# Pair 2's gather moved ahead of the overflow check, mean squares taken in column groups, and one more pair of experts stored and gathered, in a one-core hybrid decoder block

## The chip, the cores and the metric

The kernel runs on one core of a Trainium2 chip. The metric is the device time of one execution in microseconds (us). The kernel before took 687.26 us, the median of three runs (685.65 to 687.46). The profile is of one execution, in which every instruction of the five engines has a record: PE (TensorE, the matmuls; PEld is its weight load), DVE (VectorE), ACT (ScalarE), POOL (GpSimd) and SP (SyncE, which here issues DMAs and computes nothing).

## The reference, cut to what matters

One decoder layer works on 512 tokens of width 1024, in float32:

```
h = rms_norm(x);  z = h @ w_in                      # 1024 x 4864
y_r = retention(...) @ w_ret_o;  q, k = rms_norm per head of 64;  y_s = swa(q, k, v) @ w_swa_o
x = x + (sigmoid(gate_r) * y_r + sigmoid(gate_s) * y_s) @ w_out
x = x + sum over the token's 2 experts of w * (silu(n @ Wg) * (n @ Wu)) @ Wd   # n = rms_norm(x)
x = x + sigmoid(rms_norm(x) @ w_ple_gate) * rms_norm(p @ w_ple)
```

There are 32 experts of width 256. Each token goes to two of them, so there are 1024 pairs of a token and an expert, 64 on average for two experts. The per-head norms of q (8 heads) and k (2 heads) need the mean square over 64 columns of each of 10 heads.

## The kernel before, in words

**First part (0 to about 310 us).** The projections run as "units" of 128 columns with three matmuls for each block of 128 inputs (a rounded high part and a low remainder of both operands, `mm_T`, L441). A planner orders the instructions of this part by its own costs. Attention (`swa`, L534) and retention are generators whose steps are laid between the units. The first step of `swa` sums the squares of q and k over each head: five matmuls (L540) with the squares of two heads each write into the same 10 partitions of a PSUM bank, DVE copies the 10 rows out (L544), PE transposes them (L546, four blocks), DVE adds epsilon (L550), and POOL raises the 2 k columns and the 8 q columns to the power -0.5 (L554, L555). Two matmul rows later (L562) PE spreads the k factors.

**From L1104 on** the order of the instructions on every engine is the written order of the program; nothing is reordered, and an engine that waits holds everything behind it.

**Router and expert pairs.** Experts are handled in 16 pairs (p and p + 16). Each of the two has 64 slots, so a pair has 128 rows. For a pair, in this order: `gu` (L1187) multiplies the pair's rows by gate and up weights, with the two experts in the two halves of PE's columns (L1195); `hidden` (L1204) makes silu times up; `ht` (L1212) transposes it (L1216); `turn` (L1080) transposes the rows of the next pair (L1087), which an indirect DMA on POOL has gathered from X1 in DRAM (`fetch`, L1071, DMA on L1076), and then issues the gather of two pairs ahead; `turned` puts the norm's gain on them (DVE, L976); `down` (L1224) multiplies by the down weights (L1239). The weights, 6 MB for a pair, come by DMAs that SP issues in one fixed order as slabs of SBUF come free (`pump`, L310; the DMAs are L336 and L338). They go around eight semaphores in turn.

**Overflow check.** In pair 0, between `gu(0)` and `hidden(0)`, `overflow` (L1325) reads the largest number of tokens of an expert into a register (L1333, L1337) and branches: where an expert has over 64 tokens, the rest is worked off in a loop; here the branch isn't taken. The block inside uses some slabs as scratch: unit 8 for its weights (`wb`), and units 0 and 4, which hold the weights `gu(1, 1)` and `gu(17, 1)`, and so are loaded again at the block's end. When the branch isn't taken, SP waits in turn for each of the eight semaphores and raises it by what the block would have added (nine event instructions on L1337). `fetch(1)` stands ahead of the check. `fetch(2)` writes unit 8 and stands behind the check (L1565).

**Bringing results back to the tokens.** Pairs 0 to 11 (`SC = 12`) are stored: the 128 rows of `down` go to DRAM by an indirect DMA (L1259). At pair 12, `collect` (L1512) clears eight buffers on POOL (L1517) and gathers each token's stored rows (L1522, eight indirect DMAs); rows of pairs not stored are skipped. POOL adds the two rows of a token (`presum`, L1529), for blocks 0 and 1 at the end of pair 13, for blocks 2 and 3 at the end of pair 14; DVE adds them to the residual (`total`, L1534), for blocks 0 and 1 at the end of pair 14, and for 2 and 3 in the tail. Pairs 12 to 15 are "combined" instead: `down` rounds its rows into a high and a low part (L1249, L1250), DVE builds a one-hot matrix (L1232), and in the next pair PE multiplies both parts by it for each of four token blocks (`combine`, L1269: 4 matmuls a block, 16 a pair), and DVE adds the bank to the residual (`added`, L1282). Block 3 of pair 14 is combined in the tail with block 3 of pair 15.

**Tail.** For each token block: `combine([15], t)` and, for blocks 2 and 3, `total`; `tail_a` transposes the residual on PE (L1449) and splits it (L1451, L1453, L1455); `tail_b` multiplies by the gate weights (L1475); `tail_c` ends the block and stores it. The gate weights are split ahead of that (`wpsplit`, L1419) in four pieces: ACT makes the high part (L1427) and POOL, for the first three pieces, the low part (L1429), two POOL instructions a piece. Pieces 0 and 1 come in pair 15, piece 2 behind `tail_a(0)`. The written order at the seam is:

```
down(15); total / presum of that pair, if any
combine([15], 0); tail_a(0); wpsplit(2); combine([15], 1); tail_b(0, 0); wpsplit(3)
```

Of the kernel before, what the change touches and what calls it, by code (L numbers as in the profile page):

```python
# [13 lines left out]
OP = mybir.AluOpType  # L14
AX = mybir.AxisListType

P = 128
# [10 lines left out]
def constants():  # L28

    p = np.arange(P, dtype=np.float64)  # L30
    lg = np.log1p(-np.exp2(-5.0 - np.arange(4)))
    parts = []

    def add(name, a):
        a = np.broadcast_to(np.asarray(a, dtype=np.float64), (P,) + np.shape(a)[1:])
        parts.append((name, a.reshape(P, -1)))

    add("id", np.eye(P))
    add("mh", np.full((P, 40), -0.5))
    add("blk", np.stack([np.stack([((p // 64) == m - 2 * i) / 64.0 for m in range(10)], 1) for i in range(5)], 1))  # L40
    add("ones", np.ones((P, P)))
    add("up", (p[:, None] < p[None, :]) * 1.0)
    ij = p[None, :] >= p[:, None]
    dk = 128.0 ** -0.5
    rm = (np.stack([np.where(ij, np.exp(-(p[:, None] + 1) * lg[h]), 0.0) * dk for h in range(4)], 1))
    xi = np.tile(np.stack([np.exp((p + 1) * lg[h]) for h in range(4)])[None], (P, 1, 1))
    add("zeta", np.stack([np.exp((127.0 - p) * lg[h]) * dk for h in range(4)], 1))
    add("io64", (np.arange(SLOTS) + 1.0)[None])
    add("io32", np.arange(NE)[None] * 1.0)
    add("dst", np.stack([k * S + t * P + p - BIG for k in range(2) for t in range(4)], 1))  # L50
    off, o = {}, 0
    for n, a in parts:
        off[n] = (o, o + a.shape[1])
        o += a.shape[1]
    tab = np.concatenate([a for _, a in parts], 1).astype(np.float32)
    q = np.arange(P)
    s = np.arange(2 * P)
    rel = q[:, None] + P - s[None, :]
    ok = (rel >= 0) & (rel < P)
    sl = np.exp2(-np.arange(1, 9, dtype=np.float64))  # L60
    bias = np.stack([np.where(ok, -sl[h] * rel, -1e30) for h in range(8)], 1).astype(np.float32)
    return tab, off, bias, rm.reshape(P, 512).astype(np.float32), xi.reshape(P, 512).astype(np.float32)
# [136 lines left out]
def program(tc, I, out):  # L199
    nc = tc.nc  # L200
    V, A, T, G, Q = nc.vector, nc.scalar, nc.tensor, nc.gpsimd, nc.sync
# [18 lines left out]
    def C(name, a=0, b=None):  # L220
        lo, hi = CO[name]
        return ct[:, lo + a: hi if b is None else lo + b]
# [27 lines left out]
    LN = 256  # L250
    FW = ((0, 1), ), ((1, 2), (2, 4))
    TB0 = 0
    SC = 12
    KEEP = {7: (42, 50), 9: (42, 74)}
    AT = {("gu", 1, 0): 14, ("gu", 17, 0): 18, ("gu", 1, 1): 0, ("gu", 17, 1): 4}
    LATE = (("gu", 17, 1),)
# [277 lines left out]
    def swa():  # L534
# [1 line left out]
        qH, qL, kraw, vS = z["qH"], z["qL"], z["kraw"], z["vS"]  # L536
        aH, aL = ar.get(8, r=True), ar.get(8, r=True)
        pm, p2 = bgb(), bgb()
        for i in range(5):
            T.matmul(pm[0:10, :], C("blk", 10 * i, 10 * i + 10), sq2[i].f(512), start=(i == 0), stop=(i == 4))  # L540
        for s_ in sq2:
            s_.free()
        mr = ar.get(2, "t")
        V.tensor_copy(mr.f(512)[0:10, :], pm[0:10, :])  # L544
        for t in range(4):
            T.transpose(p2[:, t * 10:t * 10 + 10], mr.f(4, P)[0:10, t, :], ident[0:10, 0:10])  # L546
        mr.free()
        r = small(40)
        rk_ = small(8)
        V.tensor_tensor(r.rearrange("p (t c) -> p t c", t=4), p2[:, 0:40].rearrange("p (t c) -> p t c", t=4),  # L550
                        em[:, :, None].to_broadcast([P, 4, 10]), op=OP.add)
        rv4, rk4 = r.rearrange("p (t c) -> p t c", t=4), rk_.rearrange("p (t c) -> p t c", t=4)
        mh = C("mh", 0, 40).rearrange("p (t c) -> p t c", t=4)
        G.tensor_tensor(rk4, rv4[:, :, 8:10], mh[:, :, 8:10], op=OP.pow)  # L554
# [724 lines left out]
    def added(t):  # L1279
        for nh in range(2):  # L1280
            xs = x2[t].f(1024)[:, nh * 512:(nh + 1) * 512]
            V.tensor_tensor(xs, xs, CB[t][nh], op=OP.add)  # L1282
# [41 lines left out]

    def overflow():  # L1325

        spill = [(key, loaded.pop(key)) for key in (("gu", 1, 1), ("gu", 17, 1))]
        for _, a in spill:
            a.free()
        gm, tb_, xg, h, xr, wb = (ar.get(kb, r=r, at=at) for kb, r, at in (  # L1330
            (2, True, 0), (4, False, 1), (4, False, 4), (2, False, 3), (4, False, 6), (4, False, 8)))
        o = xr
        count = lambda ap: nc.values_load(ap, min_val=0, max_val=S, skip_runtime_bounds_check_because=(  # L1333
            "a token counts once for an expert, so 512 is the most"))
# [203 lines left out]
    for p_ in range(16):  # L1538
# [6 lines left out]
        if p_ == 0:  # L1545
            gu(0, range(2))
            post_e(2), post_e(3)
            for t in range(4):
                G0[t].free()
            tables()  # L1550
            fetch(1)
            counts()
            gu(0, range(2, 4))
        else:
            gu(p_, range(4))
# [6 lines left out]
            overflow()  # L1562
        hidden(p_)
        if p_ == 0:
            fetch(2)  # L1565
            ht(0)
            down(0)
            pump(0)
            turned(1, turn(1))
            continue  # L1570
# [4 lines left out]
        ht(p_)  # L1575
        if p_ > SC:
            added(2)
        turned(p_ + 1, turn(p_ + 1))
        for t in range(4):
            if PU[t] == p_:  # L1580
# [28 lines left out]
    tail_c(0, 1)  # L1609
    for t in range(1, 4):  # L1610
        if t < 3:
            combine([15] if t == 1 else [14, 15], t + 1)
            total(t + 1)
        tail_b(t, 0)
        tail_c(t, 0)
        if t < 3:
            tail_a(t + 1)
            tail_r(t + 1)
        for lo in range(0, 512, 512 if t < 3 else LN):
            tail_b(t, 1, lo, 512 if t < 3 else LN)  # L1620
            tail_c(t, 1, lo, 512 if t < 3 else LN)
# [59 lines left out]
```

## Time and profile before

| | |
|---|---|
| median of the runs shown | 687.26 us |
| the profiled execution's own time | 686.33 us |
| its span, first to last instruction | 684.6 us |
| PE busy | 649.4 us (95%) |
| PEld, DVE, ACT, POOL busy | 440.2, 317.0, 201.4, 99.1 us |
| DMA | 162.98 MB, mean 238 GB/s |
| granted PE clock, mean over the span | 0.995 of full speed |

A span is the time from the first to the last instruction. Times in the rows below are us from the span's start, unless a mean of one instruction is given in ns. A row of a timeline has the start, the time, the engine, the line, the operation, the tiles written and read, the shape and the count of merged instructions; in brackets stands the idle time before it and what ended that. Line numbers are those of the kernel before.

### The profile page before, as it was taken

To read this page: it belongs to the slowest core of one execution; us is meant where nothing else is said; L and a number is where in the kernel's file an instruction comes from. 1 tells how busy PE (TensorE), PEld (TensorE's weight loads), DVE (VectorE), ACT (ScalarE), POOL (GpSimd) and SP (SyncE) were. 2 spreads that over 40 slices of the span, in tenths; PEclk is the share of its full clock that TensorE was granted. 3 is DMA by queue.
4 is the path that set the end of the run, shared out by engine and by line. 5 is a ranking of instruction groups with operands and counts; after the bars stand their busy time and mean duration, and the time that the engine had idled before them with its cause. 6 is when DMAs were issued, how large, how long until landed. Compare 5 with 4: busy or idle time off the path is not lost. (4 is left out here: it accounts for less than half of the span.)

```text
span 684.6 us, 8420 instructions
## 1 busy us (share of the span) xinstructions
PE 649.4 (95%) x3210; PEld 440.2 (64%) x3210; DVE 317.0 (46%) x689; ACT 201.4 (29%) x393; POOL 99.1 (14%) x83
## 2 busy tenths in 40 slices
PE   8999999999999999999998879899999999898997
PEld 6868888778888888888888323333333443344886
DVE  5595545662456425634157312222122236565863
ACT  6764253462143334440142000000211110005431
POOL 2014000000001000000000021111421118226300
PEclk9999999999999999999999989999999999999999
DMA  8727310531304731045899759999999999994011
GB/s 279 302 78 277 108 62 2 183 124 63 117 20 170 309 123 62 0 185 202 354 402 371 287 185 371 418 419 419 421 421 419 376 423 417 417 416 197 32 47 46
DMA packets 32476, 162.98 MB, mean 238 GB/s; under 512 B 5577, under 2 KB 8265, under 8 KB 16304
## 3 DMA queue, kind: packets, MB, share of 16 engines
q1 hardware_dynamic: 26672, 149.90, 55.5%
q0 software_dynamic: 5040, 10.39, 4.0%
q10 hardware_dynamic: 720, 2.11, 0.8%
q8 instruction: 26, 0.43, 0.2%
q14 instruction: 18, 0.15, 0.1%
HBM read 155.67 MB, written 14.68 MB: 249 GB/s over the span
## 5 line engine op out<-in xcount | busy, mean ns | idle before, releaser
L445 PE MATMUL bank<-slab,slab 128*128 128x512 f32 x320 | 126.3, 395 | 0.0
L446 PE MATMUL bank<-slab,slab 128*128 128x512 f32 x320 | 125.0, 391 | 0.0
L447 PE MATMUL bank<-slab,slab 128*128 128x512 f32 x320 | 124.9, 391 | 0.0
L1195 PE MATMUL bank<-slab,slab 128*64 128x512 f32 x512 | 121.4, 595 | 2.2 <-issue 1.0
L1195 PEld LDWEIGHTS bank<-slab,slab 128*64 128x64 f32 x512 | 37.9, 137 | 78.9 <-issue 70.0
L362 DVE TENSOR_TENSOR slab<-slab,slab 128x1024 fp32r<-128x1024 f32 (+2 forms) x50 | 54.0, 1093 | 57.2 <-ACT slab L361 42.4
L445 PEld LDWEIGHTS bank<-slab,slab 128*128 128x128 f32 x320 | 60.1, 188 | 13.9 <-issue 1.8
L447 PEld LDWEIGHTS bank<-slab,slab 128*128 128x128 f32 x320 | 60.1, 188 | 12.8 <-DVE slab L362 0.3
L446 PEld LDWEIGHTS bank<-slab,slab 128*128 128x128 f32 x320 | 60.2, 188 | 11.7
L1239 PE MATMUL bank<-slab,slab 128*64 128x512 f32 x256 | 61.3, 612 | 2.3 <-DMA slab<-wd 1.7
L361 ACT ACTIVATE slab<-slab 128x1024 fp32r<-128x1024 f32 (+2 forms) x50 | 46.4, 952 | 56.7 <-PE bank L446 25.4
L1209 DVE SCALAR_TENSOR_TENSOR slab<-slab,st,bank 128x256 f32<-128x256 f32 x16 | 7.7, 480 | 99.9 <-ACT slab L1208 99.9
L1208 ACT ACTIVATE slab<-bank,st 128x256 f32<-128x256 f32 x16 | 7.6, 474 | 138.1 <-PE bank L1195 130.4
L1475 PE MATMUL bank<-slab,slab 128*128 128x512 f32 (+1 forms) x216 | 45.3, 368 | 0.0
L1475 PEld LDWEIGHTS bank<-slab,slab 128*128 128x128 f32 x216 | 37.1, 189 | 6.8 <-ACT slab L1453 0.3
L1239 PEld LDWEIGHTS bank<-slab,slab 128*64 128x64 f32 x256 | 18.6, 140 | 34.5 <-issue 32.2
L1076 POOL DMA_INDIRECT slab<-X,st x15 | 15.5, 1034 | 83.0 <-PE bank L1195 49.7
L369 POOL TENSOR_TENSOR st<-st,ct 128x4 f32<-128x4 f32 x4 | 4.4, 1102 | 159.3 <-DVE st L368 159.3
L894 PE MATMUL bank<-slab,slab 128*128 128x512 f32 x64 | 26.1, 408 | 0.0
L896 PE MATMUL bank<-slab,slab 128*128 128x512 f32 x64 | 25.0, 391 | 0.0
L895 PE MATMUL bank<-slab,slab 128*128 128x512 f32 x64 | 24.9, 390 | 0.0
L1252 DVE COPY slab<-bank 128x512 f32<-128x512 f32 x12 | 8.3, 692 | 32.0 <-PE bank L1239 32.0
(248 smaller groups left out, 926.4 us busy)
## 6 DMA issues: line engine op xcount, KB each, us to landing
slab<-wgu SPq DMA_DIRECT2D x64, 1024.0 KB, 14.8
slab<-wd SPq DMA_DIRECT2D x31, 1024.0 KB, 16.5
slab<-win SPq DMA_DIRECT2D x17, 1024.0 KB, 4.9
slab<-x SPq DMA_DIRECT2D x8, 512.0 KB, 6.2
Y<-slab SPq DMA_DIRECT2D x8, 512.0 KB, 5.4
slab<-wout SPq DMA_DIRECT2D x4, 1024.0 KB
slab<-wpg SPq DMA_DIRECT2D x4, 1024.0 KB, 22.4
slab<-wso SPq DMA_DIRECT2D x2, 1024.0 KB, 6.6
```

The lines of the kernel that those rows point to most:

```text
L361: A.activation(H.r(*shape), rawap, AF.Copy)
L362: (eng or V).tensor_tensor(L.r(*shape), rawap, H.f(*shape), op=OP.subtract)
L445: T.matmul(ps, wh[:, k, :], hh[k], start=(k == 0), stop=False)
L446: T.matmul(ps, wh[:, k, :], hl[k], start=False, stop=False)
L447: T.matmul(ps, wl[:, k, :], hh[k], start=False, stop=(k == nk - 1))
L894: T.matmul(ps, a, wh[:, kk, :], start=(k == 0), stop=False)
L895: T.matmul(ps, a, wl[:, kk, :], start=False, stop=False)
L896: T.matmul(ps, b, wh[:, kk, :], start=False, stop=(k == 7))
L1076: G.indirect_dma_start(out=XR[p_].f(1024), out_offset=None, in_=X1, in_offset=bass.IndirectOffsetOnAxis(ap=toki[:, p_:p_ + 1], axis=0), bo ...
L1195: T.matmul(b[j * 64:(j + 1) * 64, :], xg[:, k, j * 64:(j + 1) * 64], load(("gu", p_ + 16 * j, k // 4)).f(4, 512)[:, k % 4, :], start=(k == ...
L1239: T.matmul(bs[nh][j * 64:(j + 1) * 64, :], t.f(2, P)[:, f, j * 64:(j + 1) * 64], load(("wd", p_ + 16 * j)).f(2, 1024)[:, f, nh * 512:(nh + ...
L1475: T.matmul(b, (H, L, H)[i][:, k, :], w, start=(k, i) == terms[0], stop=(k, i) == terms[-1])
```

## The change

`SC` becomes 13: pair 12 is stored like pairs 0 to 11, `collect` and the building of `io` move to pair 13, `presum` of blocks 0 and 1 to pair 14, and `total` of blocks 0 and 1 and `presum` of blocks 2 and 3 to the end of pair 15 (these stand at `SC + 1` and `SC + 2`). Pairs 13, 14 and 15 are combined. Block 3 of pair 14 is combined in pair 15, ahead of `down(15)`. `fetch(2)` stands behind `fetch(1)`, ahead of the check; the check's scratch for weights goes from unit 8 to unit 14, so that `gu(1, 0)`, which lies there, is a third weight that the block would load again. The mean squares are written to four groups of columns, 32 partitions apart, and the sums of k are added to rows 2 and 3 of the first group.

```
-    add("blk", ... for m in range(10)], 1) for i in range(5)], 1))
+    add("blk", ... for m in range(4)], 1) for i in range(2)], 1))
-    SC = 12
+    SC = 13
...
-        for i in range(5):
-            T.matmul(pm[0:10, :], C("blk", 10 * i, 10 * i + 10), sq2[i].f(512), start=(i == 0), stop=(i == 4))
+        for i in range(4):
+            T.matmul(pm[32 * i:32 * i + 4, :], C("blk", 0, 4), sq2[i].f(512), start=True, stop=(i > 0))
+        T.matmul(pm[0:4, :], C("blk", 4, 8), sq2[4].f(512), start=False, stop=True)
...
-        V.tensor_copy(mr.f(512)[0:10, :], pm[0:10, :])
+        V.memset(mr.f(512), 0.0)
+        for i in range(4):
+            V.tensor_copy(mr.f(512)[32 * i:32 * i + 4, :], pm[32 * i:32 * i + 4, :])
         for t in range(4):
-            T.transpose(p2[:, t * 10:t * 10 + 10], mr.f(4, P)[0:10, t, :], ident[0:10, 0:10])
+            T.transpose(p2[:, t * P:(t + 1) * P], mr.f(4, P)[:, t, :], ident)
...
-        V.tensor_tensor(r..., p2[:, 0:40]..., em..., op=OP.add)
+        V.tensor_tensor(r4_[:, :, 0:8]..., p4...[:, :, :, 0:2], em..., op=OP.add)
+        V.tensor_tensor(r4_[:, :, 8:10], p4[:, :, 2:4], em..., op=OP.add)
...
-        spill = [(key, loaded.pop(key)) for key in (("gu", 1, 1), ("gu", 17, 1))]
+        spill = [(key, loaded.pop(key)) for key in (("gu", 1, 1), ("gu", 17, 1), ("gu", 1, 0))]
-            (2, True, 0), (4, False, 1), (4, False, 4), (2, False, 3), (4, False, 6), (4, False, 8)))
+            (2, True, 0), (4, False, 1), (4, False, 4), (2, False, 3), (4, False, 6), (4, False, 14)))
...
-            fetch(1)
+            fetch(1), fetch(2)
             counts()
...
         hidden(p_)
         if p_ == 0:
-            fetch(2)
             ht(0)
...
         if p_ > SC:
             added(2)
+        if p_ == 15:
+            combine([14], 3)
         turned(p_ + 1, turn(p_ + 1))
...
-            combine([15] if t == 1 else [14, 15], t + 1)
+            combine([15], t + 1)
```

## Rows read from the trace of the kernel before

**Rows 1.** Busy time of each engine in five stretches (us), then the granted PE clock as a share of 2.4 GHz, the busy share of the 16 DMA engines, and GB/s.

```profile
391.00:411.00 20.00, 14.74 (x60) 5.68 (x62) 3.19 (x6) 1.07 (x2) 4.03 (x4) 0.83 0.57 203
402.20:408.90 6.70, 5.12 (x16) 2.57 (x18) 1.38 (x2) 0.00 (x0) 2.03 (x2) 0.50 0.35 107
440.00:460.00 20.00, 17.77 (x92) 6.97 (x90) 5.08 (x9) 1.55 (x3) 3.04 (x3) 1.00 1.02 419
600.00:620.00 20.00, 18.79 (x80) 9.13 (x79) 11.92 (x20) 3.57 (x6) 4.63 (x3) 1.00 1.02 416
620.00:640.00 20.00, 18.36 (x79) 11.64 (x80) 15.17 (x20) 10.31 (x16) 15.42 (x7) 1.00 0.22 90
```

**Rows 2.** Timeline of PE over pairs 1 and 2: gate and up (L1195), the transposes of the hidden rows (L1216), of the next pair's rows (L1087), and down (L1239).

```profile
391.36 7.09 PE L1195 MATMUL bank<-slab,slab 128*64 128x512 f32 x32 [0.36 <-DVE slab L976]
399.58 0.44 PE L1216 MATMUL bank<-ct,slab 128*128 128x128 f32 x2 [1.14 <-DVE slab L1209]
403.78 1.97 PE L1087 MATMUL bank<-ct,slab 128*128 128x128 f32 x8 [3.76 <-DMA slab<-X,st]
405.68 5.26 PE L1239 MATMUL bank<-slab,slab 128*64 128x512 f32 x16
410.77 7.03 PE L1195 MATMUL bank<-slab,slab 128*64 128x512 f32 x32
418.93 0.44 PE L1216 MATMUL bank<-ct,slab 128*128 128x128 f32 x2 [1.12 <-DVE slab L1209]
419.20 1.04 PE L1087 MATMUL bank<-ct,slab 128*128 128x128 f32 x8
420.17 3.65 PE L1239 MATMUL bank<-slab,slab 128*64 128x512 f32 x16
423.65 0.60 PE L1195 MATMUL bank<-slab,slab 128*64 128x512 f32 x2
```

**Rows 3.** Timeline of POOL in the same time: the gathers of pairs 1 and 2 (L1076) and the store of pair 0 (L1259).

```profile
380.08 1.21 POOL L1076 DMA_INDIRECT slab<-X,st  x1 [11.30 <-DVE st L1062]
395.55 0.99 POOL L1076 DMA_INDIRECT slab<-X,st  x1 [14.27 <-SPq L1337]
396.85 1.01 POOL L1259 DMA_INDIRECT Y<-slab,st  x1 [0.31 <-issue]
```

**Rows 4.** SP's event instructions at the check: count, ns of one, first and last start.

```profile
L1337 SPq EVENT_SEMAPHORE  x9: 17/17/17, 386.1 to 394.7; - x9
```

**Rows 5.** Groups of instructions by line and shape (busy us, mean ns of one, idle us before and what ended it), and of one memset its ns; the rows of the mean squares and of the nearest like operations.

```profile
L540 PE MATMUL bank<-slab,ct 128*10 128x512 f32 x10 | 4.6, 593 | 0.0
L1195 PE MATMUL bank<-slab,slab 128*64 128x512 f32 x512 | 121.4, 595 | 2.2 <-issue 1.0 <-DMA slab<-wgu 0.8 <-DVE slab L976 0.4
L546 PE MATMUL bank<-ct,slab 10*128 10x10 f32 x4 | 0.4, 208 | 0.0
L622 PE MATMUL bank<-ct,slab 128*128 128x128 f32 x56 | 8.0, 279 | 0.0
L544 DVE COPY slab<-bank 10x512 f32<-10x512 f32 x1 | 0.7, 678 | 0.1
L351 DVE MEMSET slab<- x1: 272/272/272, 0.9 to 0.9; 128x256 f32 x1
L564 DVE SCALAR_TENSOR_TENSOR slab<-slab,st,bank 128x512 f32<-128x512 f32 x1 | 0.7, 746 | 4.2 <-PE bank L562 4.2
```

**Rows 6.** The DMA queue of POOL's indirect transfers (15 gathers of rows, 12 stores, 8 gathers of stored rows): packets, MB, share of 16 engines' span.

```profile
q0 software_dynamic: 5040, 10.39, 4.0%
```

**Rows 7.** The combining matmuls as a group, and the timeline of PE from `down(15)` into the tail, with the combine of pairs 14 and 15 for block 3.

```profile
L1269 PE MATMUL bank<-slab,slab 128*128 128x512 f32 x64 | 18.7, 418 | 0.2 <-DVE slab L1250 0.2
621.07 1.04 PE L1239 MATMUL bank<-slab,slab 128*64 128x512 f32 x2 [1.53 <-DMA slab<-wd]
622.31 3.65 PE L1239 MATMUL bank<-slab,slab 128*64 128x512 f32 x14 [0.19 <-DMA slab<-wd]
627.37 0.49 PE L1269 MATMUL bank<-slab,slab 128*128 128x512 f32 x1 [0.22 <-DVE slab L1250]
627.97 1.34 PE L1449 MATMUL bank<-ct,slab 128*128 128x128 f32 x8
642.07 1.07 PE L1269 MATMUL bank<-slab,slab 128*128 128x512 f32 x4
655.21 1.98 PE L1269 MATMUL bank<-slab,slab 128*128 128x512 f32 x8
```

**Rows 8.** Timelines of DVE and POOL from the end of pair 14 into the tail: `presum` (L1529), `total` (L1534), the low parts of the gate weights (L1429, on either engine), and the adding of pair 15's block 0 (L1282 at 627.23).

```profile
606.63 2.38 POOL L1529 TENSOR_TENSOR slab<-slab,slab 128x1024 f32<-128x1024 f32 x1 [4.82 <-DMA slab<-Y,st]
609.42 2.35 DVE L1534 TENSOR_TENSOR slab<-slab,slab 128x1024 f32<-128x1024 f32 x2
619.56 9.63 POOL L1429 TENSOR_TENSOR slab<-slab,slab 128x1024 fp32r<-128x1024 f32 x4 [10.55 <-PE bank L1216]
627.23 1.36 DVE L1282 TENSOR_TENSOR slab<-slab,bank 128x512 f32<-128x512 f32 x2
631.78 5.75 POOL L1429 TENSOR_TENSOR slab<-slab,slab 128x1024 fp32r<-128x1024 f32 x2 [2.58 <-issue]
633.57 5.03 DVE L1429 TENSOR_TENSOR slab<-slab,slab 128x1024 fp32r<-128x1024 f32 x2 [0.95 <-ACT slab L1427]
```

More of the change, by code (lines that the diff above doesn't have):

```diff
@@ L39, in constants @@
     add("mh", np.full((P, 40), -0.5))
-    add("blk", np.stack([np.stack([((p // 64) == m - 2 * i) / 64.0 for m in range(10)], 1) for i in range(5)], 1))
+    add("blk", np.stack([np.stack([((p // 64) == m - 2 * i) / 64.0 for m in range(4)], 1) for i in range(2)], 1))
     add("ones", np.ones((P, P)))
@@ L549, in swa @@
         rk_ = small(8)
-        V.tensor_tensor(r.rearrange("p (t c) -> p t c", t=4), p2[:, 0:40].rearrange("p (t c) -> p t c", t=4),
-                        em[:, :, None].to_broadcast([P, 4, 10]), op=OP.add)
+        p4, r4_ = p2.rearrange("p (t c) -> p t c", t=4), r.rearrange("p (t c) -> p t c", t=4)
+        V.tensor_tensor(r4_[:, :, 0:8].rearrange("p t (i c) -> p t i c", c=2),
+                        p4.rearrange("p t (i c) -> p t i c", i=4)[:, :, :, 0:2],
+                        em[:, :, None, None].to_broadcast([P, 4, 4, 2]), op=OP.add)
+        V.tensor_tensor(r4_[:, :, 8:10], p4[:, :, 2:4], em[:, :, None].to_broadcast([P, 4, 2]), op=OP.add)
         rv4, rk4 = r.rearrange("p (t c) -> p t c", t=4), rk_.rearrange("p (t c) -> p t c", t=4)
```

## The prediction

> **What bounds the kernel now.** I read the stretches first, then PE's timeline where PE isn't full, then the other engines there. The page has PE at 95%, but that share mixes three limits. Up to about 360 us PE has no gap worth naming, so work taken off PE counts there. From pair 1's end to about 622 us the weights set the pace: the DMA engines are full and move 416 to 419 GB/s [rows 1], and `down(15)` starts only when its weights land, with PE idle for 1.53 us [rows 7]. PE is busy for 18.8 of 20 us beside that, so the two limits lie close together. After 622 us DMA falls to 90 GB/s [rows 1], the weights are there, and PE is the bound again: in the tail every wait of PE counts.
>
> The one large hole is in pair 1. PE waits 3.76 us for gathered rows, and then works at half clock [rows 2]: the granted clock is 0.50 from 402.2 to 408.9 us, that is 1.2 instead of 2.4 GHz, and it fell while PE was idle [rows 1]. DMA moves only 203 GB/s from 391 to 411 us [rows 1], since slabs come free only when `down(1)` has read them.
>
> **Part 1, the second gather.** POOL issues pair 1's gather at 380.08 and pair 2's only at 395.55, after 14.27 us of waiting for SP's instruction on L1337 [rows 3]. Those are the nine events with which SP leaves the check, the last at 394.7 [rows 4]: each waits until the earlier weight loads on its semaphore have landed, and the gather needs them all because it writes a slab that the check's block writes. Ahead of the check it needs none of them: issued at about 381.4 us and as long under way as now (395.55 to 403.78, 8.2 us), it lands near 390, and PE wants it at 399.9. So pair 1 ends as pair 2 does. From the transposes of the hidden rows to the next pair's first matmul, pair 2 takes 423.65 - 418.93 = 4.72 us, pair 1 takes 410.77 - 399.58 = 11.19 [rows 2]: 6.47 us go, 3.76 of them the wait, 0.93 and 1.61 the two slow groups (1.97 against 1.04, 5.26 against 3.65). One cost: 64 rows of 4 KB (0.26 MB) now travel ahead of the loads that the exit waits for, 0.26 MB / 419 GB/s = 0.6 us, and `gu(1)`'s second half, due near 394.9, needs `gu(17, 1)`, released last at 394.7; up to 0.4 us. I take -6.3 (bounds -6.5 and -5). POOL's store of pair 0 also moves up, since it stood behind the gather. The slabs that `down(1)` frees come 6.3 us sooner, so the whole stream of weights starts sooner, and with the same bytes ends sooner by as much.
>
> **Part 2, pair 12 stored.** In the loop 16 of 64 combining matmuls go, 18.7 / 64 x 16 = 4.7 us of PE [rows 7], with pair 12's splitting and one-hot on ACT and DVE. The weights' stream covers it: PE would only wait longer for the next pair's weights, so I count 0 (bounds -4.7 and 0). The stored rows cost traffic in the full stream: 64 rows out and 64 back, 0.52 MB. The queue's total bears the estimate out: 15 gathers and 12 stores of 64 rows and 768 rows gathered back are 2,496 rows or 10.2 MB, against 10.39 [rows 6]. At 419 GB/s that is +1.25 us (bounds 0 and 2.5, the latter if small packets cost double). `collect` finds nothing later: POOL is free between the store of pair 12 and pair 13's turn.
>
> In the tail block 3 is combined for one pair instead of two, 1.98 - 1.07 = -0.9 us [rows 7]. The four matmuls go to pair 15 ahead of `down(15)`; there PE has 1.53 us of waiting to put them in, and they need a bank that `added(2)` frees first. I count 0 (bounds 0 and +0.7).
>
> What the change brings forward onto the path is `total`. With `SC + 2 = 15` the two additions for blocks 0 and 1, 2.35 us together where DVE has SBUF to itself [rows 8], stand at the end of pair 15, in front of `added` for pair 15's block 0, which begins at 627.23 now [rows 8]. Queued behind them on DVE are that adding and the gain of `tail_a(0)`; PE's transposes wait for the adding (they begin at 627.97, 0.1 us after the combine [rows 7]), and everything else on PE is queued behind the transposes. Nothing hides this.
>
> Nor will 2.35 us do. At that time POOL runs the low parts of the gate weights (four instructions of 2.4 us, 619.56 to 629.19), and right behind them, in the changed order, the two `presum` additions of blocks 2 and 3 (2.38 each) [rows 8]. When both engines add operands from SBUF they take turns: DVE's two of L1429 last 5.03 us while POOL runs the same, against 2.35 for two of the same size alone, and POOL's two last 5.75 against 4.8 [rows 8]. So the first `total` waits for the POOL instruction under way (0 to 2.4 us), runs 1.2, waits for POOL's next (2.4), runs 1.2: 4.8 to 7.2 us. In today's times the first would come 0.4 us after the start of POOL's fourth (629.19 - 2.4 = 626.8), so the wait is nearer the long end. I take +6.2 (bounds 2.4 and 7.2). Then PE stands idle longer than the 3.76 us in which its clock fell in pair 1. There the next 24 matmuls took 1.97 + 5.26 = 7.23 us instead of 4.69 [rows 2], 2.5 lost. I take +2.4 (bounds 0, if the clock stays, and 3.35, half of the 6.7 us of low clock in rows 1).
>
> **Part 3, mean squares.** PE now: ten matmul records, 4.6 us, 0.46 each, one after the other; with two halves of the columns side by side, L1195 takes 121.4 / 512 = 0.24 a record [rows 5]. If four strips overlap like halves, 4.6 us become 2.4; if not at all, 4.6; if all four ran at once, 1.8. The transposes get wider: four at 8.0 / 56 = 0.14, +0.2 against 0.4 [rows 5]. PE: -2.6 to +0.2. DVE gets three more copies of 0.68, a memset of about 0.54 (twice the row's 0.272) and one more addition (about 0.2) [rows 5]: +2.8 us in the chain to the k factors. Behind that chain DVE is idle for 4.2 us [rows 5], and PE has units to go on with, which the planner lays in between. That cover hides it; without it PE loses up to 2 us. I take -1.5 (bounds -2.6 and +2.0).
>
> The Trainium skill (TensorE: Matmul & The Clock Gate, "Part 3: Packing small matmuls — row/col tiling") gives 2.38 times the speed for three matmuls in strips of 32 columns; by that, as an estimate, the four would take 8 x 0.46 / 2.38 = 1.55 us and the fifth 0.9, so PE would gain 1.9 and the sum below would be 0.4 lower. No row here shows strips of 32; the halves of L1195 agree with it in kind.
>
> **Sum.** -6.3 + 1.25 - 0.9 + 6.2 + 2.4 - 1.5 = +1.15. The profiled execution took 686.33 us (its span 684.6 and 1.73 around it): 687.5. It is 0.93 under the median, so in the median's terms 688.4. Its own range, from the phase of DVE against POOL, the clock and the traffic, is 685.8 to 691.
>
> **Rivals.** *A, the seam is short.* If DVE's two additions find POOL idle or run beside it, and PE's clock stays up, the tail loses 2.4 instead of 8.6 us: 688.4 - 3.8 - 2.4 = 682.2. For it: `presum`'s inputs are long there, and POOL's four could end sooner against `down(15)`. Against: rows 8, the same shapes taking turns. 0.22.
>
> *B, PE and not DMA sets the loop.* Then the 4.7 us of combining count and the traffic doesn't: 688.4 - 4.7 - 1.25 = 682.4. For it: 18.8 of 20 us busy. Against: 416 GB/s in the same 20 us and `down(15)` waiting [rows 1, 7]. 0.07.
>
> *C, pair 1 trades one wait for another (slower).* `gu(1, 0)` now belongs to the block, so PE's first matmul of pair 1 waits for an exit event. The block issues 17 loads instead of 16 on eight semaphores; the seventeenth is on the first, whose event comes at 386.1, and PE arrives at 391.36: no wait. If it hung on the last event, 394.7, PE would wait 3.3 us and likely lose its clock again, 2.5: 688.4 + 5.8 = 694.2. It decides as soon as that event is later than 391.36. 0.10.
>
> *D, the mean squares cost.* DVE's extra 2.8 us, or another order from the planner, holds PE by 2 us instead of giving 1.5: 691.9. For it: the chain copy, transpose, addition, power stands ahead of the scores. Against: 4.2 us of idle DVE [rows 5]. 0.11.
>
> **How the numbers follow.** The forecast has 0.50. This measurement can tell 0.3% (2.06 us) from no change: faster is below 685.2, slower above 689.3. Of the forecast's 0.50, 0.03 lies below and 0.13 above. Faster 0.22 + 0.07 + 0.03 = 0.32; slower 0.10 + 0.11 + 0.13 = 0.34; the same 0.34. With cases on both sides the range is wide: 681.5 to 692 holds D and most of A and B, and leaves out C and the lower edges of A and B, about 0.2.
>
> **What would show it.** Pair 1: no wait on L1087, clock at 1.00 from 402 to 409, `gu(2)` about 6 to 8 us sooner, no wait ahead of `gu(1)` (else C). Loop: more waits on weights in pairs 13 to 15, `down(15)` ending near 620 (sooner by 4.7 more would be B). Seam: `total` twice on DVE between the last low part of `down(15)` and the adding, some 5 to 7 us long, PE idle before its transposes in the tail, a clock of 0.50 behind that. First part: records of L540's successor starting together, PE still without gaps, everything up to pair 0 sooner by 1 to 2 us. A seam under 3 us, or a clock that holds, makes the forecast wrong on the fast side; a gap in pair 1 on the slow side.

## The result, and the profile after

The changed kernel takes 696.62 us (median of 4 runs, 694.67 to 698.46) against 686.45 us before (median of 4). The ratio is 1.0146, with a 95% interval of [1.0126, 1.0166]: 10.0 us slower. The prediction was 688.4 us, in a range of 681.5 to 692.0. The profiled execution took 697.54 us, with a span of 695.8 us; before it was 684.6.

The starts of PE's rows cut both spans into stretches (us; `gu(0)`, `gu(2)` and `down(15)` are the first matmuls of these steps):

| stretch | before | after | difference | forecast |
|---|---|---|---|---|
| start to the first mean square | 42.16 | 43.24 | +1.08 | 0 |
| from there to `gu(0)` | 333.96 | 337.61 | +3.65 | -1.5 |
| `gu(0)` to `gu(2)` | 34.66 | 34.44 | -0.22 | -6.3 |
| `gu(2)` to `down(15)` | 210.30 | 211.17 | +0.87 | +1.25 |
| `down(15)` to the end | 63.48 | 69.31 | +5.83 | +7.7 |

The first line is not the change's: up to there PE runs the same instructions in both kernels (see the last section). The other four add up to 10.1 us, which is what the medians show. Two of them, from the first mean square to `gu(0)` and from there to `gu(2)`, went another way than forecast.

In the kernels with the new mean squares, line numbers behind them are 6 higher: gate and up is L1201 instead of L1195, down is L1245 instead of L1239.

**Mean squares.** Timeline of PE in the changed kernel, from the sums of squares (L540, L541) to the matmuls that spread the k factors (L568):

```profile
43.24 1.04 PE L540 MATMUL bank<-slab,ct 128*4 128x512 f32 x8
44.09 1.02 PE L541 MATMUL bank<-slab,ct 128*4 128x512 f32 x2
45.05 0.65 PE L490 MATMUL bank<-ct,slab 128*128 128x128 f32 x4
...
56.60 1.98 PE L568 MATMUL bank<-ct,st 128*64 128x128 f32 x16 [4.95 <-POOL st L560]
```

The matmuls do what they were meant to: ten records in 45.05 - 43.24 = 1.8 us, where they took 4.6 [rows 5]. But PE then stands for 4.95 us, waiting for POOL. In the kernel before it went on without a wait:

```profile
53.48 1.09 PE L562 MATMUL bank<-ct,st 128*64 128x128 f32 x16
```

The same stretch on POOL, first after and then before:

```profile
49.50 5.44 POOL L561 TENSOR_TENSOR st<-st,ct 128x32 f32<-128x32 f32 x1 [19.98 <-DVE st L557]
54.91 1.64 POOL L560 TENSOR_TENSOR st<-st,ct 128x8 f32<-128x8 f32 x1
```

```profile
49.37 2.56 POOL L554 TENSOR_TENSOR st<-st,ct 128x8 f32<-128x8 f32 x1 [20.92 <-DVE st L550]
51.90 5.43 POOL L555 TENSOR_TENSOR st<-st,ct 128x32 f32<-128x32 f32 x1
```

After the change, POOL does the q power (L561) first and the k power (L560), for which PE waits, second; before, the k power (L554) came first. The text of both kernels has the k power first, so it was the planner that exchanged them. DVE explains it in part: the q rows are now added by an instruction of their own, and first.

```profile
45.15 2.79 DVE L547 COPY slab<-bank 4x512 f32<-4x512 f32 x4
...
49.23 0.19 DVE L554 TENSOR_TENSOR st<-bank,st 128x32 f32<-128x32 f32 x1
49.34 0.16 DVE L557 TENSOR_TENSOR st<-bank,st 128x8 f32<-128x8 f32 x1
```

**Pair 1.** Timeline of PE (compare [rows 2]):

```profile
391.05 3.65 PE L1245 MATMUL bank<-slab,slab 128*64 128x512 f32 x16 [0.56 <-DVE slab L1224]
394.63 1.09 PE L1093 MATMUL bank<-ct,slab 128*128 128x128 f32 x8
400.26 9.17 PE L1201 MATMUL bank<-slab,slab 128*64 128x512 f32 x32 [4.53 <-SPq L1343]
410.56 0.44 PE L1222 MATMUL bank<-ct,slab 128*128 128x128 f32 x2 [1.13 <-DVE slab L1215]
410.83 1.04 PE L1093 MATMUL bank<-ct,slab 128*128 128x128 f32 x8
411.80 3.65 PE L1245 MATMUL bank<-slab,slab 128*64 128x512 f32 x16
415.29 4.89 PE L1201 MATMUL bank<-slab,slab 128*64 128x512 f32 x22
```

The wait for gathered rows is gone (L1093 at 410.83 follows at once, at full pace), and in its place PE waits 4.53 us ahead of `gu(1)` for SP, then takes 9.17 us for what took 7.09. The gathers are issued as planned, side by side (POOL's timeline), and SP leaves the check with its last event at 400.1 (its event instructions as a group; [rows 3, 4] are those of before):

```profile
384.80 1.21 POOL L1082 DMA_INDIRECT slab<-X,st  x1 [11.29 <-DVE st L1068]
386.31 0.99 POOL L1082 DMA_INDIRECT slab<-X,st  x1 [0.30 <-POOLq L1343]
```

```profile
L1343 SPq EVENT_SEMAPHORE  x9: 17/17/17, 390.8 to 400.1; - x9
```

**Loop.** The queue of the indirect transfers (compare [rows 6]) moved 0.49 MB more, and the loop ran 0.87 us longer. DMA is as full as before [rows 1]: it moved 416 GB/s from 425 to 600 us.

```profile
q0 software_dynamic: 5184, 10.88, 4.1%
```

**Seam.** Timelines of PE, DVE and POOL from `down(15)` on (compare [rows 7, 8]):

```profile
626.46 1.07 PE L1245 MATMUL bank<-slab,slab 128*64 128x512 f32 x2 [0.41 <-DMA slab<-wd]
...
632.83 0.49 PE L1275 MATMUL bank<-slab,slab 128*128 128x512 f32 x1 [0.23 <-DVE slab L1256]
638.75 1.97 PE L1455 MATMUL bank<-ct,slab 128*128 128x128 f32 x8 [5.43 <-DVE slab L1288]
640.37 2.06 PE L1275 MATMUL bank<-slab,slab 128*128 128x512 f32 x4
642.23 6.21 PE L1481 MATMUL bank<-slab,slab 128*128 128x512 f32 x24
```

```profile
632.69 5.41 DVE L1540 TENSOR_TENSOR slab<-slab,slab 128x1024 f32<-128x1024 f32 x2
638.02 1.27 DVE L1288 TENSOR_TENSOR slab<-slab,bank 128x512 f32<-128x512 f32 x2
```

```profile
624.22 9.52 POOL L1435 TENSOR_TENSOR slab<-slab,slab 128x1024 fp32r<-128x1024 f32 x4 [18.40 <-PE bank L1222]
633.70 6.61 POOL L1535 TENSOR_TENSOR slab<-slab,slab 128x1024 f32<-128x1024 f32 x2
```

This is the seam of the forecast: the two `total` (L1540) take 5.41 us, since POOL adds beside them: for the first 1.05 us the last of its low parts, which ends at 633.74, and then `presum` (L1535). PE waits 5.43 us. They alternate as forecast: the first `total` ends 1.0 us behind the low part, the second, 3.35 us long, has to wait for the first `presum`, and that `presum` takes 3.32 us instead of 2.38.

**The clock behind the three waits.** Busy time by engine in three stretches, then the granted clock, the DMA share and GB/s:

```profile
56.33:59.75 3.42, 3.15 (x19) 2.62 (x20) 1.11 (x2) 0.34 (x1) 0.22 (x1) 0.50 0.34 141
397.67:404.49 6.82, 4.23 (x10) 1.37 (x12) 0.00 (x0) 0.00 (x0) 1.03 (x1) 0.50 0.73 257
636.60:643.43 6.83, 4.68 (x15) 4.09 (x16) 5.96 (x9) 2.58 (x4) 3.95 (x3) 0.50 0.00 0
```

In each of the three waits the clock falls to 0.50, that is 1.2 GHz, and PE's first rows behind the wait run at it: L568 takes 1.98 us (1.09 before), `gu(1)` 9.17 (7.09), and the first rows of the tail 1.97 + 2.06 + 6.21 = 10.24 (1.34 + 1.17 + 5.78 = 8.29). Two of these rows, of the kernel before:

```profile
629.06 1.17 PE L1269 MATMUL bank<-slab,slab 128*128 128x512 f32 x4
630.12 5.78 PE L1475 MATMUL bank<-slab,slab 128*128 128x512 f32 x24
```

### The profile page after: what moved, and what is told of

Read it like the earlier page. It is cut to its first block, busy times and chain, and to the rows that moved or that the text cites. A ratio compares the mean times of both kernels' runs of the same rounds, so it can differ in the third digit from the quotient of the medians.

```text
span 695.8 us, 8384 instructions
## 1 busy us (share of the span) xinstructions
PE 647.7 (93%) x3194; PEld 440.9 (63%) x3194; DVE 312.7 (45%) x686; ACT 200.8 (29%) x392; POOL 101.3 (15%) x84
## 5 line engine op out<-in xcount | busy, mean ns | idle before, releaser
L1201 PE MATMUL bank<-slab,slab 128*64 128x512 f32 x512 | 125.4, 604 | 10.4 <-DMA slab<-wgu 4.8
L1201 PEld LDWEIGHTS bank<-slab,slab 128*64 128x64 f32 x512 | 38.9, 139 | 91.0 <-issue 76.2
L1245 PE MATMUL bank<-slab,slab 128*64 128x512 f32 x256 | 59.6, 599 | 1.2 <-DMA slab<-wd 0.7
L1245 PEld LDWEIGHTS bank<-slab,slab 128*64 128x64 f32 x256 | 18.1, 136 | 32.4 <-issue 30.2
```

The source lines that it names most:

```text
L1201: T.matmul(b[j * 64:(j + 1) * 64, :], xg[:, k, j * 64:(j + 1) * 64], load(("gu", p_ + 16 * j, k // 4)).f(4, 512)[:, k % 4, :], start=(k == ...
L1245: T.matmul(bs[nh][j * 64:(j + 1) * 64, :], t.f(2, P)[:, f, j * 64:(j + 1) * 64], load(("wd", p_ + 16 * j)).f(2, 1024)[:, f, nh * 512:(nh + ...
```

## The experiments

My theory after these rows: three separate costs, one in each place, each a wait of PE with a slow clock behind it. The rivals: a later stage hides one of them, or the cause of one is another than its row names. Twelve kernels were run: seven edit the changed kernel, five build up from the kernel before. Ratios are to the kernel before, which was run again beside each group of them. Where a time is said to be less than that of the changed kernel, medians are compared; by the ratios these differences come out 0.5 to 1.3 us larger.

### The mean squares as before, in the changed kernel

```diff
-        for i in range(4):
-            T.matmul(pm[32 * i:32 * i + 4, :], C("blk", 0, 4), sq2[i].f(512), start=True, stop=(i > 0))
+        for i in range(5):
+            T.matmul(pm[0:10, :], C("blk", 10 * i, 10 * i + 10), sq2[i].f(512), start=(i == 0), stop=(i == 4))
...
```

> The changed kernel with the mean squares as before (ten rows in one accumulation), parts 1 and 2 kept. Theory: the new mean squares cost pair 0 its start 4.7 us (380.85 against 376.12), because POOL ran the 5.44 us power of the q rows ahead of the 1.64 us power of the k rows that PE waited for (4.95 us) and PE's clock then fell; with the old ones pair 0 starts at about 376.1 and the time is about 692.0 (696.6 - 4.7). Rival: the late start has another source (the clock at 0.50 from 11.96 to 15.37 us, say), then pair 0 starts at 379 to 381 and the time is 695 to 697.

Measured: 693.0 us, ratio 1.0078 [1.0052, 1.0105]: 3.6 us less than the changed kernel. PE has no wait left there; `gu(0)` starts at 377.84. That is later than expected, but the first mean square starts later too: from there to `gu(0)` it takes 377.84 - 43.95 = 333.89 us, as in the kernel before (333.96). The 4.7 us that I expected back held 1.08 us from ahead of the change.

### The k rows added first

```diff
+        V.tensor_tensor(r4_[:, :, 8:10], p4[:, :, 2:4], em[:, :, None].to_broadcast([P, 4, 2]), op=OP.add)
         V.tensor_tensor(r4_[:, :, 0:8].rearrange("p t (i c) -> p t i c", c=2),
...
-        V.tensor_tensor(r4_[:, :, 8:10], p4[:, :, 2:4], em[:, :, None].to_broadcast([P, 4, 2]), op=OP.add)
```

> The changed kernel with DVE's two additions exchanged, so that the k rows are added first and POOL's k power stands ahead of its q power; everything else as changed. Theory, the order of the two powers is the whole cost: PE's wait of 4.95 us on POOL and the low clock behind it go, the eight matmuls side by side save their 2.6 us, pair 0 starts at 374 to 375.5 and the time is about 690.5. Rival, DVE's four copies, memset and second addition are the cost (2.8 us in the chain): a wait of 1.5 to 3 us on the k power remains, pair 0 starts at 377.5 to 379.5, the time is 693 to 695.

Measured: 690.82 us, ratio 1.0043 [1.0021, 1.0064]: 5.8 us less than the changed kernel, and 2.2 less than with the old squares. `gu(0)` starts at 375.05, and from the first mean square to there it takes 331.35 us: 6.3 less than in the changed kernel and 2.5 less than with the old squares. Timeline of POOL, and then the row of PE that waited:

```profile
49.95 1.65 POOL L560 TENSOR_TENSOR st<-st,ct 128x8 f32<-128x8 f32 x1 [19.96 <-DVE st L554]
51.56 7.54 POOL L561 TENSOR_TENSOR st<-st,ct 128x32 f32<-128x32 f32 x1
```

```profile
52.05 1.09 PE L568 MATMUL bank<-ct,st 128*64 128x128 f32 x16
```

The k power ends at 51.6, and PE, with its units in between, arrives after it: no wait, and full clock. DVE's four copies are still there, so they cost PE nothing. The order of POOL's two instructions was the whole loss, and the column groups themselves are a gain.

### The block's scratch on another slab

```diff
-        spill = [(key, loaded.pop(key)) for key in (("gu", 1, 1), ("gu", 17, 1), ("gu", 1, 0))]
+        spill = [(key, loaded.pop(key)) for key in (("gu", 1, 1), ("gu", 17, 1), ("gu", 2, 0))]
...
-            (2, True, 0), (4, False, 1), (4, False, 4), (2, False, 3), (4, False, 6), (4, False, 14)))
+            (2, True, 0), (4, False, 1), (4, False, 4), (2, False, 3), (4, False, 6), (4, False, 34)))
```

> The changed kernel with the block's weight scratch laid on the slab of gu(2,0) in place of gu(1,0); both gathers stay ahead of the check. Theory: PE's 4.53 us ahead of gu(1) is the wait of gu(1,0)'s slab for SP's leaving of the block, and the clock of 0.50 from 397.7 to 404.5 follows from it: both go, gu(2) starts 14 to 16 us behind the end of gu(0)'s down(0) work instead of 19.6, and the time is 696.6 - 4.5 - 2.5 = about 689.6. Rival 1: PE's next weights, gu(17,1), land at 400.1 and hold gu(1)'s second half, so that only half of it comes back: 693. Rival 2: every reader behind the block waits for the whole exit: no change, 696.

Measured: 692.8 us, ratio 1.0077 [1.0054, 1.0099]. In its profile `gu(0)` to `gu(2)` takes 28.20 us instead of 34.44, so 6.2 us come back in this place; its first part was 2.3 us longer than in the profile of the changed kernel, with the clock at 0.94 from 60 to 80 us where that had 1.00, so that the total shows less. PE's timeline:

```profile
398.41 7.09 PE L1201 MATMUL bank<-slab,slab 128*64 128x512 f32 x32 [0.37 <-DVE slab L982]
406.91 1.04 PE L1093 MATMUL bank<-ct,slab 128*128 128x128 f32 x8
```

No wait for the exit, none for the gather, none in the second half of `gu(1)`: neither rival held, though the time alone, 692.8, would have fitted the first.

### Two of the block's buffers exchanged

This asks which write to the slab PE waited for: the scratch's loads, or the reading again of `gu(1, 0)` at the block's end.

```diff
-            (2, True, 0), (4, False, 1), (4, False, 4), (2, False, 3), (4, False, 6), (4, False, 14)))
+            (2, True, 0), (4, False, 1), (4, False, 14), (2, False, 3), (4, False, 6), (4, False, 4)))
```

> The changed kernel with two of the block's buffers exchanged: the weight scratch, which the block's 12 weight loads write, goes on the slab of gu(17,1), and the block's gathered rows, which DVE and ACT write, on that of gu(1,0). gu(1,0) is still given up and read again by the block (the seventeenth load), so it still belongs to it. Theory: PE's 4.53 us come from the scratch's loads, which stand on all eight semaphores, not from the reload: the wait ahead of gu(1) goes, PE reaches the second half of gu(1) about 0.1 us after the last exit event, and the time is close to that of the run with the scratch on gu(2,0), about 692.8, with gu(2) 28 to 29 us behind gu(0). Rival, any slab that the block reloads waits for the last exit event: the wait of 4.5 us stays, 696.6.

Measured: 692.85 us, ratio 1.0077 [1.0051, 1.0103], level with the run above. PE's timeline:

```profile
393.56 5.35 PE L1245 MATMUL bank<-slab,slab 128*64 128x512 f32 x16 [0.56 <-DVE slab L1224]
400.29 7.09 PE L1201 MATMUL bank<-slab,slab 128*64 128x512 f32 x32 [0.36 <-DVE slab L982]
```

The wait is gone though the slab is still read again by the block. (`gu(0)` to `gu(2)` took 29.89 us, 1.7 more than above: `down(0)`, ahead of this place, ran 5.35 us instead of 3.65, with the clock at 0.73 to 0.79 from 392 to 399 us.) The program agrees: in the changed kernel PE's first matmul of `gu(1)` stands behind waits for all eight load semaphores, here for two of them. The scratch's waits now stand ahead of the first matmul on `gu(17, 1)`, in the second half of `gu(1)`, which PE reaches when the last event (402.5 us) is past.

### `total` ahead of the seam

```diff
             combine([p_ - 1], 0), combine([p_ - 1], 1)
+        if p_ == 15:
+            total(0), total(1)
...
         if p_ == SC + 2:
-            total(0), total(1)
             presum((2, 3))
```

> The changed kernel with the two additions total(0) and total(1) moved from the end of pair 15 to the place behind combine of block 1 in pair 15, where DVE is idle for 3.6 us and POOL is idle. Theory: the 5.41 us that they took while POOL's presum ran are PE's wait of 5.43 us ahead of the tail's first transposes, and the clock of 0.50 from 636.6 to 643.4 follows from it: the wait goes to under 0.5 us, the two take 2.4 us where they stand now, and the time is 696.6 - 5.2 - 2.4 = about 689. Rival: the tail then waits for the next thing, POOL's low parts of the gate weights behind presum, and only 2 to 4 us come back: 692.5 to 694.5.

Measured: 691.67 us, ratio 1.0066 [1.0044, 1.0088]: 5.0 us less than the changed kernel. `down(15)` to the end takes 64.74 us instead of 69.31, and the clock stays at 1.00 at the seam. PE's transposes begin without a wait:

```profile
633.45 1.34 PE L1455 MATMUL bank<-ct,slab 128*128 128x128 f32 x8
```

So most of the 5.83 us come back, though not the 7.6 of the theory, and a part of the rival holds: `presum` still runs on POOL at the seam, and PE has two small waits for DVE behind it (0.72 and 0.95 us).

### `presum` alone moved

```diff
             combine([p_ - 1], 0), combine([p_ - 1], 1)
+        if p_ == 15:
+            presum((2, 3))
...
             total(0), total(1)
-            presum((2, 3))
```

> The changed kernel with only POOL's two presum additions of blocks 2 and 3 moved, from behind total at the end of pair 15 to the place behind combine of block 1 in pair 15, where POOL is idle; total(0) and total(1) stay at the end of pair 15. Theory, DVE and POOL take turns at additions of two SBUF operands: with POOL's presum gone from that place, DVE's two take about 2.4 us instead of 5.41 unless a low part of POOL's is still under way, PE's wait ahead of the tail's transposes falls from 5.43 to 2.4 to 3.6 us, and the clock may hold: 696.6 - 2.5 to -5, about 692.8. Rival, the additions are long by themselves at this place (2.7 us each): the wait stays at 5.4 and the time at 696.

Measured: 694.18 us, ratio 1.0100 [1.0066, 1.0134]: 2.4 us less than the changed kernel. `down(15)` to the end takes 66.6 us instead of 69.31. Timelines of DVE, POOL and PE:

```profile
632.81 3.24 DVE L1540 TENSOR_TENSOR slab<-slab,slab 128x1024 f32<-128x1024 f32 x2
```

```profile
624.32 9.52 POOL L1435 TENSOR_TENSOR slab<-slab,slab 128x1024 fp32r<-128x1024 f32 x4 [3.58 <-PE bank L1222]
```

```profile
636.71 1.81 PE L1455 MATMUL bank<-ct,slab 128*128 128x128 f32 x8 [3.25 <-DVE slab L1288]
```

DVE's own instructions and their place are unchanged, and their time falls from 5.41 to 3.24 us. Of that, 624.32 + 9.52 - 632.81 = 1.03 us is the end of POOL's low part; from there on the two take 2.2. So they take turns with POOL; the rival, long by themselves, falls. The clock still fell behind the wait of 3.25 us.

### The three parts, each alone on the kernel before

Part 1 as changed (both gathers ahead of the check, scratch on `gu(1, 0)`):

> The kernel before with part 1 alone, as changed, with the block's scratch on gu(1,0). Theory: the wait for the exit takes the whole gain; PE waits about 4 us ahead of gu(1) and the clock falls behind it, gu(0) to gu(2) takes 34.0 to 34.7 us as in the kernel before, and the time is 686 to 687.5. Rival: since pair 0 comes 4.7 us sooner here than in the changed kernel, against weights that are loaded at their own pace, the wait is another: 2 us or less, 683, or 7 us, 690.

Measured: 686.49 us, ratio 0.9994 [0.9978, 1.0009]: no change, as the theory had it. PE's timeline:

```profile
396.67 9.37 PE L1195 MATMUL bank<-slab,slab 128*64 128x512 f32 x32 [4.40 <-SPq L1337]
```

The same part with the scratch on `gu(2, 0)`:

> The kernel before with part 1 alone, and the block's scratch on gu(2,0) in place of gu(1,0). Theory: the second gather ahead of the check gives back the 3.76 us of waiting and the slow clock behind them, gu(0) to gu(2) takes 28.2 to 28.5 us instead of 34.66 and nothing downstream gives it back: 687.5 - 6.3 = about 681. Rival: the weights' stream, which starts when slabs come free, has its own pace, and half or more of it returns as waits on weights: 684 or more.

Measured: 679.79 us, ratio 0.9896 [0.9871, 0.9922]. `gu(0)` to `gu(2)` takes 28.19 us, 6.5 less than before, and `gu(2)` to `down(15)` takes 210.15 against 210.30: the stream of weights gives nothing back.

```profile
391.73 7.09 PE L1195 MATMUL bank<-slab,slab 128*64 128x512 f32 x32 [0.36 <-DVE slab L976]
400.23 1.04 PE L1087 MATMUL bank<-ct,slab 128*128 128x128 f32 x8
```

Part 2 as changed (pair 12 stored):

> The kernel before with part 2 alone, as changed. Theory: 0.9 us of traffic in the loop (gu(2) to down(15) 211.2 instead of 210.3) and 5.8 us in the tail (69.3 instead of 63.5 from down(15) to the end), nothing else: 687.0 + 6.7 = about 693.7. Rival: with pair 1's gap where it was, the phase of DVE against POOL at the seam is another, and the cost is 3 us or less: 690.

Measured: 693.13 us, ratio 1.0087 [1.0060, 1.0114]. `gu(2)` to `down(15)` 211.01 us, `down(15)` to the end 69.00. DVE and PE at the seam:

```profile
630.10 5.37 DVE L1534 TENSOR_TENSOR slab<-slab,slab 128x1024 f32<-128x1024 f32 x2
```

```profile
636.12 1.97 PE L1449 MATMUL bank<-ct,slab 128*128 128x128 f32 x8 [5.38 <-DVE slab L1282]
```

Part 3 as changed (column groups):

> The kernel before with part 3 alone, as changed (POOL's q power ahead of its k power). Theory: this part alone costs what the start of pair 0 lost: PE's 4.95 us of waiting and a slow clock behind it, less 2.6 us of matmuls, 3 to 5.5 us in the profiles so far: 687.0 + 4.2 = about 691, with 2 to 4 us in the median between one profile and the next, as the clock falls once or twice behind the wait. Rival: the weights' stream hides it, since weights are loaded ahead during the wait: 688 or less.

Measured: 691.73 us, ratio 1.0075 [1.0046, 1.0104]. PE waits 4.95 us ahead of L568 again. From the first mean square to `gu(0)` it takes 338.89 us, 4.9 more than before; of that, 1.1 us come back between `gu(0)` and `gu(2)`, where PE waits 1.82 us for the gathered rows instead of 3.76, and nothing behind that.

The ratios of the three parts as changed give -0.4, +6.0 and +5.2 us on their common 686.7: 10.7 us together, against 10.0 for the whole change.

### All three mended, and without part 2

The first is the changed kernel with the k rows first, the scratch on `gu(2, 0)`, and `total` and then `presum` behind `combine([14], 1)`; the second the kernel before with parts 1 and 3 so mended, and pair 12 combined as it was.

> The changed kernel with all three mended: the k rows added first, the block's scratch on gu(2,0), total(0), total(1) and then presum of blocks 2 and 3 behind combine of block 1 in pair 15. Theory, the three costs are separate and add up: 696.6 - 5.8 (the k power first) - 6.2 (the scratch: gu(0) to gu(2) took 28.2 us instead of 34.4) - 4.6 (the tail from down(15): 64.7 instead of 69.3) - 1 (0.72 and 0.95 us of waits that presum still cost the tail) = 679 to 680, below the kernel before by about 1.1%. Rival: the weights' stream sets the end, and what is won ahead of it comes back as waits on weights in pairs 12 to 15: 684 to 687.

> The kernel before with parts 1 and 3 as mended (scratch on gu(2,0); k rows added first), and part 2 left out: pair 12 stays combined. Theory: part 2, with its additions at a better place, is worth nothing, since its traffic takes 1.1 us (211.26 against 210.15) and its tail gives 0.8 (62.66 against 63.49), so this kernel stands level with the one with all three mended, at 677 to 678. Rival: part 2 mended pays, and this kernel is 1.5 us or more slower: 679.

Measured: 677.38 us, ratio 0.9864 [0.9839, 0.9890], and 678.26 us, ratio 0.9875 [0.9852, 0.9898]. Both are faster than both kernels of the case, by 9.3 and 8.6 us against before. The first is about 2 us faster than expected. In its profile the clock was 1.00 from 10 to 20 us, in that of the changed kernel 0.83 (last section); whether that is the difference was not tried. PE's timeline at the seam of the first:

```profile
619.00 0.50 PE L1275 MATMUL bank<-slab,slab 128*128 128x512 f32 x1 [0.23 <-DVE slab L1256]
619.59 1.34 PE L1455 MATMUL bank<-ct,slab 128*128 128x128 f32 x8
620.69 1.18 PE L1275 MATMUL bank<-slab,slab 128*128 128x512 f32 x4
621.75 5.73 PE L1481 MATMUL bank<-slab,slab 128*128 128x512 f32 x24
```

No wait and full clock; its tail takes 62.66 us against 63.48 before, and its loop 211.26 against 210.30. So storing pair 12, done well, gives 0.8 us in the tail and takes 1.0 in the loop. The two intervals lie over one another: no run here tells part 2 from nothing.

## Why the prediction was wrong, step by step

Two of its steps failed, and each brought a wait of PE that the sum didn't hold: the cover that was to hide the chain of part 3 left out the order of POOL's two powers, and the argument against rival C looked at one load of the slab where the branch makes thirteen.

- **Mean squares, -1.5: the step failed.** It came out at +3.65 in the profile and at +5.2 alone; the five other profiles with POOL's powers in this order have +3.5 to +5.7, since the clock stays low behind the wait for longer in some. The matmuls were priced well at the lower bound (1.8 us if all four ran at once; they did), and DVE's copies were hidden, as I said (the memset isn't in the chain at all: it ran at 5.72 us). What the step left out was POOL. I counted the instructions that the edit adds, and not that it splits the one addition on which both of POOL's powers waited: before, both were ready together and k stood first; after, q's input is ready 0.1 us sooner, and the planner put the long power ahead of the short one that PE needs. That the 0.1 us decided it is inferred; that the order on POOL is the cause is shown, since exchanging two lines took it all back, and the stretch then gains 2.6 us (331.35 against 333.96). Rival D named "another order from the planner", but priced it at 2 us, from DVE's extra instructions; the price was on POOL, 5.44 us for the q power, which is not among [rows 5], and a slow clock behind it.
- **The second gather, -6.3: right by itself, eaten by rival C.** Where the exit wait is avoided, the stretch gains 6.5 us (34.66 to 28.19), within the bounds, and all of it lasts to the end. As changed, it gained 0.2, and in the other profiles with this pair 1 it takes 32.4 to 34.5 us. The failed step is the argument against rival C: "the seventeenth is on the first, whose event comes at 386.1". That load is the reading again of `gu(1, 0)`; in the program it stands on the fifth semaphore, which did no harm. But the slab is also the scratch of the block, and the block's 12 loads into it stand on all eight semaphores, so the first matmul of `gu(1)` waits for the last event. The exchange of the two buffers shows it: with the reload left and the scratch elsewhere there is no wait. Rival C's price was near: 3.3 + 2.5 us against 4.53 and 9.17 - 7.09 = 2.08. Its wait is 1.2 us longer than 3.3, and 0.7 of that is a later exit, which comes 19.3 us behind `gu(0)` (400.1 - 380.85) instead of 18.6 (394.7 - 376.12, [rows 4] and the table); 0.6 us had been named for that. All the profiles with both gathers ahead of the check have 18.8 to 19.3, those with one 18.2 to 18.6. My chance of 0.10 stood on a step that the text of the program could have settled.
- **Traffic, +1.25:** +0.87 in the changed kernel, +0.7 with part 2 alone (211.01 - 210.30), for 0.49 MB. The nine profiles with pair 12 stored have 210.98 to 211.25 us in the loop, the five others 209.99 to 210.34. The mechanism held: the weights set the loop, the 16 matmuls gone from it gave nothing, and rival B fell.
- **The seam, +6.2 and +2.4 for the clock:** 5.43 - 0.1 = 5.3 us of waiting and 10.24 - 8.29 = 1.95 us of slow clock; the combine in the tail gave -0.9 (1.07 for 1.98), as forecast. These add up to 6.4, the whole stretch to 5.83; where the other 0.5 us went was not followed. The mechanism was right, and rival A fell. The Trainium skill (SBUF — State Buffer, "Who interferes with whom") says that GpSimd shares a pair of ports with VectorE and that the sharing is an exclusive lock; this trace agrees, with 5.41 us beside POOL's low part and additions and 2.2 once POOL is out of the way.
- **The sum.** Two right terms and two wrong ones: +1.15 forecast, +10.1 found (without the 1.08 us ahead of the change). Of the 9.0 between, 5.2 are part 3, 6.1 part 1, and -2.3 the seam and the traffic, which cost less than forecast. The rivals C and D were both there with their places, but as alternatives with a chance each. They are independent of one another and of the seam, and the range had no case in which they came true together: 688.4 + 5.8 + 3.5 = 697.7 by their own prices. That this lies near the 696.62 measured is in part luck, since D was priced by another engine's work.

## What to carry to other kernels

Where a step is moved ahead of a branch by giving the branch another buffer for its scratch, list every write that the branch makes to that buffer, and look up on which semaphores these stand; whoever reads it first behind the branch waits for the latest of them, so give the branch a buffer that is read late. Where an edit splits one instruction into two, follow both halves to every engine that they feed: a planner may reorder a third engine by it. Mishaps in separate places add up, so the slow end of a range has to hold their sum.

## What the runs showed of the hardware

- Four matmuls in strips of 32 columns ran side by side: eight records of 128 x 512 within 1.04 us, the next two in 1.02, 1.8 us in all against 4.6. The Trainium skill (TensorE: Matmul & The Clock Gate, "Part 3: Packing small matmuls — row/col tiling") gives 2.38 times the speed for three strips, from which I had estimated 2.45 us; the trace shows less time than that.
- PE's clock fell behind waits shorter than the 3.76 us known from before: behind 3.25 us at the seam, and with part 1 alone in `down(15)` behind 1.52 us. The latter wait is there in the kernel before too (1.53 us, [rows 7]), without a fall. Nor does a longer wait always bring one: with `total` ahead of the seam, PE waited 2.84 us ahead of `gu(1)` and then took 7.09 us for it, at full clock, while `down(0)` ahead of that had run at 0.54 to 0.61 from 394 to 398 us behind waits of 1.17 and 0.56 us. What decides was not tried. Granted clock of the kernel with part 1 alone, as changed:

```profile
622.00:624.00 2.00, 1.85 (x6) 0.36 (x7) 1.03 (x2) 1.14 (x2) 2.00 (x2) 0.79 0.92 374
624.00:626.00 2.00, 2.00 (x8) 0.65 (x6) 0.00 (x0) 0.00 (x0) 1.92 (x2) 0.50 0.43 180
```

- From 10 to 20 us, where PE runs the same instructions in all the kernels, the granted clock was 1.00 in the profile of before and 0.83 in that of the changed kernel, and its first mean square came 1.08 us later. Of the fourteen profiles four have 1.00 (before, the gather alone with the scratch on `gu(2, 0)`, and the last two kernels) and ten 0.83; the first mean square starts at 41.8 to 42.3 us in the four and at 43.2 to 44.0 in the ten. The memset that the change adds on DVE, at 5.72 us, doesn't decide it: both values occur with it and without. What does was not tried.
